# A decoder step on one core: the computed instruction order starts at the first instruction instead of at the second stage

## The chip, the cores and the metric

One Trainium2 chip, one core of it. The metric is the device time of one execution in microseconds; the median of three runs stands for a kernel. On the core five engines work at the same time, each on its own queue of instructions and in the order of that queue: TensorE (PE, with its weight loads as PEld), VectorE (DVE), ScalarE (ACT), GpSimd (POOL) and SyncE (SP), which here only issues transfers. An instruction that waits holds up everything behind it on its engine.

## The reference, cut to what matters

One layer of a hybrid decoder, for a prompt of 1024 rows and for a decode group of 8 x 8 rows that shares the weights. Only the first part matters for the change:

```
h = rmsnorm(x, norm_mix_pre)
z = h @ w_in                          # 1024 -> 256 + 256 + 32 + 512
c_q, c_kv, k_r, u = split(z)
attn = mla(c_q, c_kv, k_r)            # decode group: 8192 cached rows per sequence, read through a page table
ssm  = s5(u)                          # complex diagonal state space, parameters from ssm_a, ssm_log_dt, ssm_b, ssm_c
x = x + rmsnorm(concat(rmsnorm(attn), rmsnorm(ssm)) @ w_out)
x = x + cross_attention(x);  x = x + conv_ffn(x)
```

## The kernel before, in words

`Kern` runs its stages one after the other. `stage_in` (L396) is the projection z = h @ w_in. The rows are nine tiles, in the order 8 (the 64 decode rows), 0, 1, ..., 7 (128 prompt rows each, every eighth row). A tile's matmuls (L488) are 24 triples, 8 slices of the 1024 inputs by three products of high and low halves, into three PSUM banks of the tag "z", of which there are six. `rows_T` (L465) loads a tile ahead: xT, which ACT and DVE split into xh and xl (L325, L326), and x, which ACT squares and sums (L356) and POOL turns into the scale r1 (L345, L346). After the matmuls ACT scales z into cz (L490), DVE copies kr_raw and u_all (L496 to L499), and these free the three banks; then cn and ckv are written and stored.

Three other pieces of work sit between the tiles. At t == 1, `q_weights` (L544) loads w_uq in two parts (staging tile "wuq"), splits them into wuqh and wuql in a pool q_s opened for that, and `query_rows` (L552) makes the decode queries q_s. At t == 2, `dec_start` (L938) opens a pool d_q, reads the page table into the row indices idx, transposes w_uk (L959) and the queries (L968), multiplies them (L981) into Ql, sends Ql through DRAM (qld, L985, L987) into Qb, and closes d_q. From t == 3 to t == 7 two pieces a tile of `gen_ssm` (L610) are traced: the state space parameters, a long chain of small DVE operations on tiles of up to 128x256 that begins with the load of prm (L625) and ends with `yield True` (L752). All banks that these use are "z" banks too, and the six go round in the order in which the code asks for them.

`stage_par` (L1194) comes next. `gen_dec` (L1005) is the decode attention, 16 steps of two sequences' pages; a step gathers its cached rows with two DMAs that POOL issues (L1027, 2 MB each; tiles rf and kf, kf in turns in the buffers d_k0 and d_k1), DVE transposes blocks of them (kT, L1049), PE makes scores (S, L1060), DVE the maximum (mx, L1081), ACT the exponentials (P, L1088), PE the transposes and the values (L1109, L1125). Between its pieces `side()` runs the rest of the state space part, the gate, memory keys, prompt queries and weights.

Two things set the order. The tile framework places every instruction by its own simulated schedule. And `Order` (L60), made in `stage_par` at L1203, remembers how many instructions exist then; its `close()` (L220) takes all later ones up to the end of `stage_par`, derives their dependences, schedules them with a table of costs (`cost`, L104) in six rounds of a forward and a backward pass, and chains the instructions of PE, DVE, ACT and POOL in the best order found. SP's transfers are not chained. For the first use of each tile it also demands that the users of all pools listed in `behind` (L48) are through: closed pools of the same memory and the same side. `stage_in` lies outside of it.

Of the kernel before, what the change touches and what calls it, by code (L numbers as in the profile page):

```python
# [41 lines left out]
class Pool:  # L42


    def __init__(self, kern, pool, bufs, space, side):
        self.kern, self.pool, self.bufs = kern, pool, bufs
        self.space, self.open = (space, side), True
        self.behind = [p for p in kern.pools if not p.open and p.space == self.space]  # L48
        kern.pools.append(self)

    def tile(self, shape, dtype, **kw):
# [3 lines left out]

    def close(self):
        self.open = False


class Order:  # L60
# [238 lines left out]
class Kern:  # L299
# [95 lines left out]

    def stage_in(self):  # L396
        nc, i, o = self.nc, self.i, self.o
        self.pers = self.pool("pers", 1, self.actx)
        pers = self.pers
        self.u_all = pers.tile([128, 32, 8, 16], F32, tag="u_all", name="u_all")  # L400
# [64 lines left out]
        def rows_T(t):  # L465

            P = 64 if t == 8 else 128
            xT, x = first if t == 8 else (load_xT(t), load_x(t))
            j = sp.tile([128, D], BF16, tag="sqj", name="sqj", bufs=1)[:P]
            xh = sp.tile([128, 8, 128], F32R, tag="xh", name="xh")[:, :, :P]  # L470
            xl = sp.tile([128, 8, 128], F32R, tag="xl", name="xl")[:, :, :P]
            for k in (0, 4):
                self.split(xh[:, k:k + 4], xl[:, k:k + 4], xT[:, k:k + 4])
            r1 = self.rstd(sp, self.sumsq(sp, x, "ss1", j=j), D, "rs1")
            return r1, xh, xl

        order = (8, 0, 1, 2, 3, 4, 5, 6, 7)
        ahead = rows_T(8)
        for n, t in enumerate(order):
            P = 64 if t == 8 else 128  # L480
            r1, xh, xl = ahead
            if n < 8:
                ahead = rows_T(order[n + 1])
            zs = [zp.tile([128, 512], F32, tag="z", name="z") for _ in groups]
            for k in range(8):
                for (lhs, rhs, a, b) in ((xh, wh, k == 0, False), (xh, wl, False, False), (xl, wh, False, k == 7)):
                    for z, (c0, c1) in zip(zs, groups):
                        nc.tensor.matmul(z[:P, :c1 - c0], lhs[:, k, :P], rhs[:, k, c0:c1], start=a, stop=b)  # L488
            cz = sp.tile([128, 512], F32, tag="cz", name="cz")[:P]
            nc.scalar.activation(cz, zs[0][:P], AF.Copy, scale=r1)  # L490
            if t == 8:
                nc.vector.tensor_scalar_mul(kr_s_raw, zs[1][:64, 0:32], r1)
                nc.vector.tensor_scalar_mul(u_sn[:, 0:240], zs[1][:64, 32:272], r1)
                nc.vector.tensor_scalar_mul(u_sn[:, 240:512], zs[2][:64, :272], r1)
            else:
                nc.vector.tensor_scalar_mul(kr_raw[:, t], zs[1][:, 0:32], r1)  # L496
                grp = lambda a: a.rearrange("p (g c) -> p g c", c=16)
                nc.vector.tensor_scalar_mul(self.u_all[:, 0:15, t], grp(zs[1][:, 32:272]), r1)
                nc.vector.tensor_scalar_mul(self.u_all[:, 15:32, t], grp(zs[2][:, :272]), r1)  # L499
            ss2 = sp.tile([128, 2], F32, tag="ss2", name="ss2")[:P]  # L500
            j = sp.tile([128, 256], BF16, tag="sqc", name="sqc", bufs=1)[:P]
            self.sumsq(sp, cz[:, :256], "", ss2[:, 0:1], j)
            self.sumsq(sp, cz[:, 256:], "", ss2[:, 1:2], j)
            r2 = self.rstd(sp, ss2, 256, "rs2")
            cn = sp.tile([128, 512], F32, tag="cn", name="cn")[:P]
            nc.scalar.activation(cn[:, :256], cz[:, :256], AF.Copy, scale=r2[:, 0:1])
            ckv = self.ck_s if t == 8 else cn[:, 256:]
            natj = lambda a: a.rearrange("(c j) d -> j c d", j=8)[t]
            nc.vector.scalar_tensor_tensor(ckv, cz[:, 256:], r2[:, 1:2], g_kv[:P], op0=OP.mult, op1=OP.mult)
            if t == 8:  # L510
                nc.sync.dma_start(o["kv_s"], ckv)
                lat8 = cn, ckv
            else:
                nc.sync.dma_start(natj(o["kv_p"]), ckv)
                nc.sync.dma_start(natj(self.lat), cn)
                self.rope(sp, (kr_rot[:, t, 0:16], kr_rot[:, t, 16:32]), (kr_raw[:, t, 0:16], kr_raw[:, t, 16:32]),
                          csP[:, 0, t], csP[:, 1, t], [16])
            if t == 0:
                sample_lat(*lat8)
            if t == 1:  # L520

                qctx = ExitStack()
                qp = self.pool("q_s", 1, qctx, side="right")
                w = self.q_weights(qp, qp)
                self.q_s = pers.tile([64, 768], F32, tag="qy", name="q_s")
                self.query_rows(qp, [zp.tile([128, 512], F32, tag="z", name="z") for _ in range(2)], self.q_s,
                                self.cqTh_s, self.cqTl_s, *w, self.csS[:, 0], self.csS[:, 1])
                qctx.close()
            zbank = lambda: zp.tile([128, 512], F32, tag="z", name="z")
            if t == 2:  # L530
                self.dec_start(zbank)
                self.ssm_groups, opened = self.gen_ssm(zbank), False
            if 2 < t < 8:
                for _ in range(2):
                    opened = opened or next(self.ssm_groups)
        while not opened:
            opened = next(self.ssm_groups)
        nc.sync.dma_start(o["kr_p"].rearrange("(c j) r -> c j r", j=8), kr_rot)
# [1 line left out]
        self.dump("u_all", self.u_all)  # L540
        self.dump("u_sn", self.u_sn)


    def q_weights(self, wp, sp):  # L544
        wh, wl = (wp.tile([128, 2, 768], F32R, name="wuq" + z) for z in "hl")
        for k in range(2):
            st = sp.tile([128, 768], F32, tag="wuq", name="wuq", bufs=1)
            self.nc.sync.dma_start(st, self.i["w_uq"][k * 128:(k + 1) * 128])
            self.split_gain(wh[:, k], wl[:, k], st, self.col("q", k))
        return wh, wl  # L550
# [18 lines left out]
    def gen_q(self):  # L569

        nc, i = self.nc, self.i
        self.qd = self.pool("qd", 1, space=DRAM).tile([1024, 768], F32, name="qd")
        self.ckd = self.pool("ckd", 1, space=DRAM).tile([2, 128, 2, 1024], F32, name="ckd")
        ctx = ExitStack()
        sp = self.pool("q2_s", 1, ctx)
        pp = self.pool("q2_p", 2, ctx, space=PSUM)
        wh, wl = self.q_weights(sp, sp)
        bank = lambda: pp.tile([128, 512], F32, tag="ps", name="ps")
        csN = sp.tile([128, 2, 8, 16], F32, name="csN")
        nc.sync.dma_start(csN, i["k_rope_n"])  # L580
        yield
        for t in range(8):
            ts = slice(t * 128, (t + 1) * 128)
            lat = sp.tile([128, 4, 128], F32, tag="lat", name="lat", bufs=1)
            nc.sync.dma_start(lat.rearrange("p k n -> p (k n)"), self.lat[ts])
            ps = bank().rearrange("p (k n) -> p k n", k=4)
            for k in range(4):
                nc.tensor.transpose(ps[:, k], lat[:, k], self.ident)
            h, l = (sp.tile([128, 4, 128], F32R, tag="c" + z, name="c" + z, bufs=1) for z in "hl")
            self.split(h, l, ps)  # L590
            for z, a in ((0, h), (1, l)):
                nc.sync.dma_start(self.ckd[z, :, :, ts], a[:, 2:4].bitcast(F32))
            yield
            q = sp.tile([128, 768], F32, tag="q", name="q", bufs=2)
            self.query_rows(sp, (bank(), bank()), q, h, l, wh, wl, csN[:, 0, t], csN[:, 1, t])
            nc.sync.dma_start(self.qd[ts], q)
            yield
        ctx.close()
# [339 lines left out]
    def dec_start(self, bank):  # L938
# [1 line left out]
        nc, i = self.nc, self.i  # L940
        V, G = nc.vector, nc.gpsimd
        c1 = self.d_c
        ctx = ExitStack()
        sp = self.pool("d_q", 1, ctx, side="right")

        pt_i = sp.tile([128, 32], I32, name="pt_i")
        nc.sync.dma_start(pt_i, i["ptab"])
# [46 lines left out]
        ps = bank()  # L994
        nc.tensor.transpose(ps[:32, :64], self.kr_s, self.ident[:64, :64])
        V.tensor_copy(self.ckT_s[:, 8], ps[:32, :64])
        ctx.close()

    def stage_decopen(self):
        ctx = self.dctx  # L1000
# [193 lines left out]
    def stage_par(self):  # L1194

        def side():
            yield from self.ssm_groups
            yield from self.gen_glu()
            yield from self.gen_memkv()
            yield from self.gen_q()  # L1200
            yield from self.gen_attw()

        self.order = Order(self)  # L1203
        other = side()
        for _ in self.gen_dec():
            with self.tc.high_priority(100):
                next(other, None)
        for _ in other:
            pass
        self.order.close()  # L1210
        self.dctx.close()
# [1022 lines left out]
```

## Time and profile before

| | us |
|---|---|
| median of three runs (1981.37 to 1987.07) | 1987.0 |
| the profiled execution | 1987.95 |
| its span, first to last instruction | 1986.1 |
| PE busy in the span | 1846.4 |
| DVE busy | 1109.6 |
| ACT busy | 807.4 |
| POOL busy | 514.4 |

Busy time is an average over stages with different limits. In the windows below, PEclk is the TensorE clock that was granted, as a share of 2.4 GHz, and a busy PE at 0.5 does half as much. In a timeline row the bracket gives the idle time of the engine before the instruction and what ended it.

### The profile page before, as it was taken

Reading aid. Unit: us, or ns where it says so; the run is one execution under the profiler, and the core shown is the slowest. Engines: PE = TensorE matmul, PEld = TensorE weight load, DVE = VectorE, ACT = ScalarE, POOL = GpSimd, SP = SyncE. Lnnn points to the kernel's source line nnn. Section 1 sums busy time; section 2 is a strip of 40 time slices with the busy share of each in tenths; the row PEclk is TensorE's granted clock in tenths of the full one; section 3 lists DMA queues with packets and bytes.
Section 4 is the critical chain, followed back from the end, with each engine's and each line's share of the span. In section 5 each row is a group of like instructions: output and inputs, shape, how many; then the busy total and the mean of one; then the engine's idle time right before and its main releaser. Section 6 shows DMA issues by size and latency. Waiting matters only on the chain.

```text
span 1986.1 us, 31961 instructions
## 1 busy us (share of the span) xinstructions
PE 1846.4 (93%) x12675; PEld 1450.1 (73%) x12675; DVE 1109.6 (56%) x2013; ACT 807.4 (41%) x1598; POOL 514.4 (26%) x550
## 2 busy tenths in 40 slices
PE   8977898789899989999989989999999999999997
PEld 6864445346465578877868868888878999999776
DVE  4359889865646678864255563434544543334433
ACT  5232323234332368764254454333443333333342
POOL 2231111041130024234311023122144421110654
PEclk9887989899899999999999999999999999999999
DMA  7723533453575531231143352333333522222221
GB/s 239 224 72 116 203 113 130 169 214 130 192 271 204 200 94 28 78 137 50 43 138 117 138 191 95 98 101 98 97 105 106 165 86 86 86 85 79 75 85 59
DMA packets 136597, 248.07 MB, mean 125 GB/s; under 512 B 26912, under 2 KB 91232, under 8 KB 132352
## 3 DMA queue, kind: packets, MB, share of 16 engines
q1 hardware_dynamic: 129120, 170.01, 27.2%
q0 software_dynamic: 7328, 76.03, 10.0%
q8 instruction: 100, 1.64, 0.3%
q14 instruction: 49, 0.40, 0.1%
HBM read 217.26 MB, written 27.42 MB: 123 GB/s over the span
## 4 chain that ended last, share of the span: by engine, by line
PE 62%; ACT 2%; DVE 2%; issue 1%; POOL 1%; DMA 1%; SPq 0%; DVEq 0%; ACTq 0%; POOLq 0%
PE ps L2092 26%; PE z L1597 5%; PE ps L335 4%; PE ps L337 4%; PE ps L336 4%; PE b L1752 2%; PE t L1400 1%; PE S L1060 1%; PE ov L1125 1%; PE o L1416 1%; PE o L1417 1%; PE s L1378 1%; PE s L1379 1%; PE s L1380 1%; PE b L335 1%
## 5 line engine op out<-in xcount | busy, mean ns | idle before, releaser
L2092 PE MATMUL ps<-xTl,wh 128*128 128x288 f32 (+1 forms) x1056 | 287.9, 327 | 0.0
L2092 PE MATMUL ps<-xTh,wh 128*128 128x288 f32 (+1 forms) x1056 | 287.7, 327 | 0.0
L2092 PE MATMUL ps<-xTh,wl 128*128 128x288 f32 (+1 forms) x1056 | 287.7, 327 | 0.0
L326 POOL TENSOR_TENSOR wl<-st,wh 128x1024 fp32r<-128x1024 f32 (+1 forms) x52 | 116.7, 2245 | 408.0 <-ACT wh L325 397.7
L326 DVE TENSOR_TENSOR wl<-st,wh 128x1024 fp32r<-128x1024 f32 (+1 forms) x52 | 64.0, 1231 | 249.8 <-ACT wh L325 247.3
L325 ACT ACTIVATE wh<-st 128x1024 fp32r<-128x1024 f32 (+1 forms) x104 | 102.6, 993 | 235.4 <-PE ps L2092 215.2
L2092 PEld LDWEIGHTS ps<-xTl,wh 128*128 128x128 f32 x1056 | 179.6, 188 | 13.9
L2092 PEld LDWEIGHTS ps<-xTh,wl 128*128 128x128 f32 x1056 | 179.5, 188 | 13.8
L2092 PEld LDWEIGHTS ps<-xTh,wh 128*128 128x128 f32 x1056 | 179.6, 188 | 13.7
L1060 PE MATMUL S<-kT,Qb 32*64 32x512 f32 x2304 | 163.1, 641 | 27.0 <-DVE kT L1049 20.3
L326 DVE TENSOR_TENSOR wdl<-std,wdh 128x1024 fp32r<-128x1024 f32 x44 | 100.4, 2282 | 147.3 <-ACT wdh L325 147.3
L1049 DVE STREAM_TRANSPOSE kT<-kf 128x1024 f32<-128x1024 f32 x128 | 152.4, 1222 | 32.5 <-DMA kf<-in_cache_kv_dram,idx 22.9
L2043 POOL TENSOR_TENSOR al<-act,ah 128x1024 fp32r<-128x1024 f32 x44 | 106.8, 2428 | 174.0 <-ACT ah L2042 174.0
L335 PE MATMUL ps<-wdh,ah 128*128 128x512 f32 x352 | 139.5, 396 | 0.0
L336 PE MATMUL ps<-wdl,ah 128*128 128x512 f32 x352 | 139.1, 395 | 0.0
L1125 PE MATMUL ov<-kf,PT 128*64 128x256 f32 x1024 | 126.6, 394 | 0.7 <-ACT PT L1110 0.7
L337 PE MATMUL ps<-wdh,al 128*128 128x512 f32 x352 | 126.1, 396 | 0.0
L1125 PEld LDWEIGHTS ov<-kf,PT 128*64 128x64 f32 x1024 | 70.6, 141 | 54.6 <-issue 15.1
L1060 PEld LDWEIGHTS S<-kT,Qb 32*64 32x64 f32 x2304 | 46.6, 136 | 84.8 <-issue 40.0
L2042 ACT ACTIVATE ah<-act 128x1024 fp32r<-128x1024 f32 (+1 forms) x44 | 49.0, 1113 | 142.1 <-PE ps L336 136.9
L335 PEld LDWEIGHTS ps<-wdh,ah 128*128 128x128 f32 x352 | 66.2, 188 | 17.4 <-issue 0.8
L1027 POOL DMA_INDIRECT kf<-in_cache_kv_dram,idx x32 | 33.3, 1040 | 175.1 <-PE ov L1125 169.3
(536 smaller groups left out, 3945.9 us busy)
## 6 DMA issues: line engine op xcount, KB each, us to landing
st<-in_w_gate_dram SPq DMA_DIRECT2D x22, 1024.0 KB
st<-in_w_up_dram SPq DMA_DIRECT2D x22, 1024.0 KB
std<-in_w_down_dram SPq DMA_DIRECT2D x44, 512.0 KB
x<-in_x_prompt_dram SPq DMA_DIRECT2D x16, 512.0 KB
x<-x2d SPq DMA_DIRECT2D x15, 512.0 KB
wst<-in_w_in_dram SPq DMA_DIRECT2D x8, 528.0 KB
xT<-in_xT_dram SPq DMA_DIRECT2D x8, 512.0 KB
ws<-in_w_out_dram SPq DMA_DIRECT2D x8, 512.0 KB
```

The lines of the kernel that those rows point to most:

```text
L325: nc.scalar.activation(hi, src, AF.Copy)
L326: (lo_eng or nc.vector).tensor_sub(lo, src, hi.bitcast(F32))
L335: mm(ps, lh, rh, start=start, stop=False)
L336: mm(ps, lh, rl, start=False, stop=False)
L337: mm(ps, ll, rh, start=False, stop=stop)
L1049: V.transpose(t, RF[n] if kb == 8 else KF[n][:, :, :, kb * 32:kb * 32 + 32])
L1060: nc.tensor.matmul(SS[n][half[a], j], Qb[q, kb, 2 * p + a], ts[q, a], start=kb == BLOCKS[0], stop=kb == BLOCKS[-1])
L1125: nc.tensor.matmul(ov[half[a]], PTS[n, g][:, m, half[a]], KF[n][:, a, g * 4 + m], start=g == 0 and m == 0, stop=g == 3 and m == 3)
L1597: nc.tensor.matmul(z[n], l, r[:, n * 512:(n + 1) * 512], start=a, stop=b)
L2042: nc.scalar.activation(ah[:, :, :nt], a[:, :, :nt], AF.Copy)
L2043: G.tensor_sub(al, a[:, :, :512], ah[:, :, :512].bitcast(F32))
L2092: nc.tensor.matmul(zt[:, :c1 - c0], l[:, k], r[:, k, c0:c1], start=a, stop=b)
```

## The change

`self.order = Order(self)` moves from `stage_par` to the first line of `stage_in`, so that the computed order covers both stages. `behind` no longer looks at the side of a pool. A class `Slab` cuts tiles as slices out of one tile, and `slab()` asks for that tile in the buffer "kf" of pool d_k0, which the first gather of cached rows will fill later. The split query weights and all temporaries of `dec_start` now lie in such slabs, and pool d_q is gone. The staging of w_uq shares the one-buffer ring "x" with the row loads of `rows_T`. `gen_ssm` is created before the loop and gives one piece after every tile from the third on (n > 1, which is t == 1) in place of two after each from t == 3 on.

```
-        self.behind = [p for p in kern.pools if not p.open and p.space == self.space]
+        self.behind = [p for p in kern.pools if not p.open and p.space[0] == self.space[0]]
...
+class Slab:
+    def __init__(self, tile):
+        self.flat, self.off, self.tags = tile, 0, {}
+    def tile(self, shape, dtype, tag=None, name=None, bufs=1):
+        key, n = tag or name, math.prod(shape[1:])
+        if key not in self.tags:
+            self.tags[key] = self.flat[:shape[0], self.off:self.off + n]
+            self.off += n
...
     def stage_in(self):
+        self.order = Order(self)
...
+        zbank = lambda: zp.tile([128, 512], F32, tag="z", name="z")
+        self.ssm_groups, opened = self.gen_ssm(zbank), False
...
-                w = self.q_weights(qp, qp)
+                w = self.q_weights(self.slab(F32R), sp, "x")
...
-                self.ssm_groups, opened = self.gen_ssm(zbank), False
-            if 2 < t < 8:
-                for _ in range(2):
-                    opened = opened or next(self.ssm_groups)
+            if n > 1:
+                opened = opened or next(self.ssm_groups)
...
+    def slab(self, dtype=F32):
+        t = self.d_k[0].tile([128, 2, 16, 256], dtype, tag="kf", name="slab", bufs=1)
+        return Slab(t.rearrange("p a m r -> p (a m r)"))
...
-    def q_weights(self, wp, sp):
+    def q_weights(self, wp, sp, tag):
-            st = sp.tile([128, 768], F32, tag="wuq", name="wuq", bufs=1)
+            st = sp.tile([128, 1024], F32, tag=tag, name="wuq", bufs=1)[:, :768]
...
     def dec_start(self, bank):
-        ctx = ExitStack()
-        sp = self.pool("d_q", 1, ctx, side="right")
+        sp = self.slab()
...
-        ctx.close()
...
     def stage_par(self):
-        self.order = Order(self)
```

## Rows read from the trace of the kernel before

**Rows 1.** The page, section 1: busy us (share of the span) and instructions of each engine
```profile
PE 1846.4 (93%) x12675; PEld 1450.1 (73%) x12675; DVE 1109.6 (56%) x2013; ACT 807.4 (41%) x1598; POOL 514.4 (26%) x550
```

**Rows 2.** Windows, one a stage: length, busy us (instructions) of each engine, PEclk, DMA share, GB/s
```profile
0.00:140.50 140.50, 120.92 (x731) 106.35 (x731) 59.13 (x191) 54.03 (x107) 37.06 (x99) 0.94 0.58 182
140.50:697.00 556.50, 479.13 (x4773) 273.00 (x4772) 412.40 (x734) 181.77 (x449) 95.04 (x103) 0.92 0.49 175
697.00:1986.00 1289.00, 1246.34 (x7172) 1070.76 (x7172) 638.04 (x1091) 571.59 (x1043) 382.35 (x348) 0.99 0.30 97
```

**Rows 3.** Timeline of PE to 120 us: start, us, instruction, count, idle time before
```profile
8.42 1.14 PE L488 MATMUL z<-winh,xh 128*64 128x512 f32 x3 [8.42 <-ACT winh L330]
...
60.58 1.03 PE L959 MATMUL z<-ident,wuk 128*128 128x128 f32 x8
...
66.82 4.07 PE L981 MATMUL z<-qnT,wukT 64*128 64x64 f32 x29 [4.82 <-DVE qnT L971]
...
76.31 0.64 PE L488 MATMUL z<-winh,xh 128*128 128x512 f32 x3
76.79 0.65 PE L488 MATMUL z<-winl,xh 128*128 128x512 f32 x3
...
118.73 0.57 PE L488 MATMUL z<-winh,xh 128*128 128x272 f32 x1 [6.13 <-DVE u_all L498]
```

**Rows 4.** Timeline of ACT around 62 us
```profile
62.24 1.06 ACT L356 ACTIVATE sqj<-x 128x1024 bf16<-128x1024 f32 x1 [3.84 <-DMA x<-in_x_prompt_dram]
...
64.33 0.67 ACT L490 ACTIVATE cz<-z,rs 128x512 f32<-128x512 f32 x1
```

**Rows 5.** Windows about the three PE gaps and behind them, columns as before
```profile
61.90:75.80 13.90, 9.08 (x58) 8.35 (x57) 3.73 (x11) 6.31 (x15) 4.31 (x12) 0.63 0.97 358
...
112.60:123.50 10.90, 4.77 (x20) 4.58 (x20) 7.50 (x28) 3.54 (x9) 5.59 (x14) 0.69 0.05 17
...
140.50:149.07 8.57, 0.64 (x5) 0.45 (x5) 5.61 (x13) 3.33 (x10) 2.95 (x10) 0.68 0.39 115
149.07:176.40 27.33, 22.25 (x228) 12.53 (x228) 25.41 (x52) 2.50 (x7) 6.64 (x6) 0.60 0.53 185
176.40:360.00 183.60, 158.03 (x1638) 88.44 (x1638) 168.95 (x343) 60.61 (x167) 23.40 (x29) 0.93 0.40 143
```

**Rows 6.** Timeline of DVE, first and last operations of the parameter chain, first transposes
```profile
92.00 0.15 DVE L627 TENSOR_SCALAR nsgn<-prm 128x1 f32<-128x1 f32 x1 [19.85 <-DMA prm<-in_ssm_par_dram]
...
117.96 0.24 DVE L496 TENSOR_SCALAR kr_raw<-z,rs 128x32 f32<-128x32 f32 x1
...
147.69 1.24 DVE L1049 STREAM_TRANSPOSE kT<-rf 128x1024 f32<-128x1024 f32 x1
...
164.71 9.10 DVE L1049 STREAM_TRANSPOSE kT<-kf 128x1024 f32<-128x1024 f32 x8
```

**Rows 7.** Timeline of SP's transfers
```profile
71.97 0.37 SPq L985 DMA_DIRECT2D qld<-Ql  x1
79.66 1.80 SPq L987 DMA_DIRECT2D Qb<-qld  x4
81.56 0.65 SPq L625 DMA_DIRECT2D prm<-in_ssm_par_dram  x1
```

**Rows 8.** Timeline of POOL: a scale alone, the first kf gather's second half, a scale beside the chain
```profile
20.29 0.55 POOL L346 TENSOR_TENSOR rs<-rs1t,neghalf 128x1 f32<-128x1 f32 x1
...
62.26 0.94 POOL L1027 DMA_INDIRECT kf<-in_cache_kv_dram,idx  x1 [0.30 <-issue]
...
96.95 1.00 POOL L346 TENSOR_TENSOR rs<-rs1t,neghalf 128x1 f32<-128x1 f32 x1
```

**Rows 9.** Up to 720 us: a DVE wait (total, times, longest), kf's landing, the maxima
```profile
DVE kT L1049 <- DMA kf<-in_cache_kv_dram,idx: 22.9, 7, 6.1
...
DMA to landing us min/median/max: 8.1/12.9/15.2
...
L1081 DVE TENSOR_REDUCE mx<-S x16: 2252/2291/2293, 176.4 to 678.3; 128x1 f32<-128x2048 f32 x16
```

More of the change, by code (lines that the diff above doesn't have):

```diff
@@ L57, in close @@
         self.open = False
+class Slab:
[6 more added lines that the diff above has]
+            self.off += n
+            assert self.off <= self.flat.shape[1]
+        v = self.tags[key]
+        if len(shape) > 2:
+            dims = "abcd"[:len(shape) - 1]
+            v = v.rearrange(f"p ({' '.join(dims)}) -> p {' '.join(dims)}", **dict(zip(dims, shape[1:])))
+        return v if dtype == self.flat.dtype else v.bitcast(dtype)
 class Order:
@@ L528, in stage_in @@
                 qctx.close()
-            zbank = lambda: zp.tile([128, 512], F32, tag="z", name="z")
             if t == 2:
                 self.dec_start(zbank)
-                self.ssm_groups, opened = self.gen_ssm(zbank), False
-            if 2 < t < 8:
-                for _ in range(2):
-                    opened = opened or next(self.ssm_groups)
+            if n > 1:
+                opened = opened or next(self.ssm_groups)
         while not opened:
@@ L576, in gen_q @@
         pp = self.pool("q2_p", 2, ctx, space=PSUM)
-        wh, wl = self.q_weights(sp, sp)
+        wh, wl = self.q_weights(sp, sp, "wuq")
         bank = lambda: pp.tile([128, 512], F32, tag="ps", name="ps")
```

## The prediction

> **What bounds the kernel now.** I read the page first: PE is busy for 1846.4 of 1986.1 us and no other engine for more than 56% [rows 1]. So time is to be had only where PE stands idle or runs at the lower clock. Windows by stage then say where that is [rows 2]. Behind 697 us, where the change touches nothing, PE is idle for 43 of 1289 us at a clock of 0.99. The projection (to 140.5 us) leaves 19.6 us idle at 0.94, and the planned stage (140.5 to 697) leaves 77.4 us idle at 0.92. The change can win only in these two.
>
> The timeline of PE shows the projection's idle time as three pieces [rows 3]: 8.42 us at the start, until the first weights have come; 4.82 us ahead of 66.82; 6.13 us ahead of 118.73. A fourth lies at the seam: in the 8.57 us up to the first scores at 149.07 PE is busy for 0.64 [rows 5]. Behind a gap PE runs at the lower of its two levels, 1.2 and 2.4 GHz: the windows about the three gaps have a granted clock of 0.63, 0.69 and 0.68 [rows 5]. At the upper one a triple of the projection follows the next after 0.48 us, as at 76.31 and 76.79 [rows 3].
>
> Each gap has a reason in the order, not in a lack of data. At 62.24 ACT sums the squares of a row tile that is needed only much later, and waits 3.84 us for its load; the split xh and the scaling cz, which frees the bank, stand behind it on ACT, cz at 64.33 [rows 4], and on DVE the copies to wukT and qnT stand behind the xl that follows xh. At 118.73 PE waits for u_all: DVE takes up kr_raw only at 117.96, because the parameter chain, which could not begin before prm came at 92.00, is ahead of it [rows 6]. prm was issued at 81.56, behind Qb, which had waited for qld since 71.97 [rows 7]. At the seam DVE does parameter tables first and turns the first gathered block at 147.69 [rows 6]; the rows it turns were gathered at about 60 us [rows 8]. The plan could not know: it takes up at the seam and has the gather start there.
>
> **The change, part by part.** All sums are against the profiled execution, 1987.95 us; its span is 1986.1, so 1.85 us lie around it. It is 1 us above the median of 1987.0.
>
> *The gap at 62 us.* The plan now covers ACT and DVE here and knows that cz and qnT are due earlier than a square sum. Removed: 4.82 us of idle, and the half speed behind it. The 9.08 busy us of that window [rows 5] lie between 66.82 and 76.31 but for a little; at half speed they lose 4.5 us if all of it goes with the clock. The small products of 64 columns, 4.07 us and more of it [rows 3], may not, so the loss is 2.1 to 4.5 and I take 3.3. Sum 8.1. Not all goes: the six banks go round, so the fourth bank of `dec_start` needs tile 2's first bank, which cz frees in 0.67 us [rows 4], then the first product must be evacuated. I leave 1.5 us standing. Gain 6.6.
>
> *The gap at 118 us.* prm is now asked for at t == 1, before `dec_start`, a tile and all of `dec_start` earlier, and the chain, 26 us long from 92.00 to 117.96 with other work in it [rows 6], is spread over six tiles. Removed: 6.13 us, and behind it most of the window's 4.77 busy us at half speed [rows 5], 2.3. Gain 8.4. If DVE still held up one tile's copies, at most the same 8.4 would stay.
>
> *The seam.* The plan now has the gathered rows in place and the engines in their true state. The first block can be turned as soon as the last matmul gives up the projection's weights, in whose place the tile lies: u_all, one transpose of 1.24 us [rows 6] and the first scores, 2.5 us. Of the 7.9 idle us there [rows 5], 5.4 go.
>
> *Query weights through the ring "x".* Both loads now stand behind a square sum of 1.06 us [rows 4] and a load of x; an estimate from these is 2 to 5 us later. What they serve in the end, the work of `dec_start`, began on PE at 60.58, behind tile 2's matmuls [rows 3]. Cost nothing, since 11.6 us of tile 2 (24 triples of 0.48 us) cover it; without that cover it is us for us, 2 to 5 us.
>
> *The first kf gather moves behind `dec_start`.* Its buffer now holds the slabs until qld has read Ql. That transfer is waited for until 79.66 after its issue at 71.97 [rows 7], so with the gap gone the buffer is free at about 72 us instead of before 61. With two issues and the longest landing of 15.2 us [rows 9] the rows are there by 90, and the first use lies at 125 or later. Cost nothing, under 35 us of cover. While POOL waits for qld, the scales of the next tile queue behind it; a wrong guess of the plan costs them up to 7 us once, and the second set of three banks hides 11.6. I take nothing, bound 7.
>
> *The rest of the planned stage* is planned anew from another start. In the 27.33 us behind 149.07 PE was busy 22.25 us at a clock of 0.60 [rows 5], while the nine blocks of the first step waited: eight were turned only from 164.71 on [rows 6], though long there. If they go first, up to 5.1 us idle and 8.9 us of clock come back, 14 in all. But DVE was busy for 169 of the next 183.6 us [rows 5], so what is moved ahead there pushes other work back. I take nothing, and bound it by a gain of 14 and by the losses below.
>
> Sum: 6.6 + 8.4 + 5.4 = 20.4 us. The profile would then show 1967.5, the median 1967.
>
> *One rule against the change.* The scale of a tile takes POOL 0.55 us at 20.29 and 1.00 us at 96.95, beside the chain on DVE [rows 8], and the chain will now lie beside six tiles. The Trainium skill, page "SBUF — State Buffer", section "Who interferes with whom", says that a VectorE instruction with two SBUF inputs contends with a GpSimd instruction that reads SBUF, and that the second to issue fully blocks; the trace agrees in direction, by 0.45 us an operation. If every tile's two scales and one rotary step stretch by 0.45 us on the path, six tiles lose 8 us and the median would be 1975. I hold it for unlikely, since r1 is made a tile ahead.
>
> **The rivals.** *The planned order is no tighter than the framework's* (also the case that the change does not do what it says). For: in the stretch that is planned now, PE is idle for 13.9% of the time (77.4 of 556.5), in the projection after its start for 8.5% (11.2 of 132.1) [rows 2, 3]. At 13.9% the projection's 120.9 busy us would take 140.4 instead of 132.1; with the seam's 5.4 us won, the kernel would be 3 us slower, 1990. Against: the planned stretch is idle where DVE is full or a gather lands, and the projection has neither.
>
> *The whole planned stage gets better too*, because the first step's blocks go first: 20.4 + 14, 1953.
>
> *Slower: gathers come into the open.* A gather takes 8.1 to 15.2 us to land and DVE waited for one in 7 steps, 22.9 us together, the longest 6.1 [rows 9]. If decode steps are packed more tightly ahead of the side work, a step shortens towards its gather. At 6.1 us in 10 of the 15 later steps the waits are 61 us, 38 more than now, less 20 won: 2005. It decides from 7 steps at 6.1 us, or 13 at the mean of 3.3, where it has eaten the 20 us. Against: the plan knows the transfers' length, and a step is 33.5 us long in the mean (15 steps from 176.4 to 678.3) [rows 9].
>
> **How the numbers follow.** Forecast 1967: 0.50. Better stage, 1953: 0.15. POOL held up, 1975: 0.05. No tighter, 1990 or somewhat below: 0.16. Slower, 2005: 0.14. About 0.3%, 6 us, is what a measurement of this kernel can tell from no change. Faster takes the first three, 0.70; same 0.16; slower 0.14. The range reaches down past the better case by the upper ends of the bounds, 1.2 us more lost clock at the first gap and the 1.5 and 2.5 us that I left standing, and up past the no-tighter case: 1947 to 1991. The slower case stays outside, and so does what is better than all bounds.
>
> **What would show it.** Right: the last projection matmul ends between 122 and 130 us; no PE gap over 3 us between 9 us and there; prm lands before 60; the first scores follow the last projection matmul within 4 us; the stage ends near 677. Wrong: POOL idle on the first kf gather with scales behind it; ACT waiting for a load again with cz behind it; decode steps of which most wait for kf; or a projection that ends at 125 while the stage still ends near 697, which would say that the second stage's end hangs on something else than its start.

## The result and the profile after

The kernel after takes 1955.56 us in the median of six runs (1952.82 to 1968.35), the kernel before 1985.15 beside it (1979.34 to 1991.38): a ratio of 0.9853, 95% interval 0.9833 to 0.9873. Two later series of the unchanged kernel after gave 0.9844 and 0.9872 (below), so the change is worth 25 to 31 us. The forecast was 1967. The profiled execution of after took 1952.82 us, its span is 1951.0. The page's first section:

```profile
PE 1837.9 (94%) x12675; PEld 1442.3 (74%) x12675; DVE 1105.0 (57%) x2013; ACT 806.9 (41%) x1598; POOL 522.5 (27%) x550
```

PE does the same 12675 matmuls in 8.5 us less than in [rows 1], and is idle for 113 us in place of 140. Windows cut at the same two places as [rows 2], the last projection matmul and the transfer of krd that ends the planned stage (columns as there):

```profile
0.00:138.40 138.40, 121.92 (x731) 105.85 (x731) 61.12 (x194) 55.50 (x113) 38.21 (x103) 0.95 0.59 186
138.40:664.50 526.10, 469.31 (x4772) 266.34 (x4772) 406.18 (x727) 180.11 (x442) 103.45 (x100) 0.94 0.52 185
664.50:1950.90 1286.40, 1246.67 (x7172) 1070.09 (x7172) 637.74 (x1094) 571.33 (x1043) 380.86 (x348) 0.99 0.31 97
```

The projection, from which 15 us were to come, is 2.1 us shorter (140.5 to 138.4). The second stage, from which 5.4 were to come at the seam (the place where the projection ends and the planned stage begins), is 30 us shorter (556.5 to 526.1); two more profiles of after have 538.5 and 535.7 for it, and the mean of the three gives 23 us in place of 30. In the last, 1289.0 and 1286.4 us, PE's busy time is the same.

**The projection.** The timeline of PE, with the rows before which it waited and those at the seam:

```profile
7.87 1.14 PE L510 MATMUL z<-winh,xh 128*64 128x512 f32 x3 [7.87 <-ACT winh L349]
28.93 0.69 PE L510 MATMUL z<-winh,xh 128*64 128x512 f32 x3 [2.37 <-ACT winh L349]
30.29 0.88 PE L510 MATMUL z<-winl,xh 128*64 128x512 f32 x3 [0.66 <-DVE winl L350]
72.78 4.06 PE L1004 MATMUL z<-slab 64*128 64x64 f32 x29 [4.65 <-DVE slab L994]
138.07 0.29 PE L510 MATMUL z<-winh,xl 128*128 128x272 f32 x1
138.95 0.66 PE L812 MATMUL ps<-ident,u_all 128*128 128x128 f32 x4 [0.59 <-DVE u_all L521]
141.28 0.64 PE L1082 MATMUL S<-kT,Qb 32*64 32x512 f32 x1
```

Beside [rows 3]: the wait of 6.13 us for u_all is gone. The wait of 4.82 us ahead of the products with w_uk is still there with 4.65, six microseconds later. And 3.0 us of waiting for the first weights' split are new, at 28.93 and 30.29.

The wait of 4.65 us ends with a copy of DVE, the queries' from a PSUM bank into the slab (L994). PE's transposes of the queries, which that copy reads, and DVE's operations from the first parameter operation to the copy:

```profile
66.70 0.46 PE L991 MATMUL z<-ident,slab 64*128 64x64 f32 x4
```

```profile
63.65 0.18 DVE L668 TENSOR_SCALAR ek<-prm 128x32 f32<-128x32 f32 x1 [2.01 <-DMA prm<-in_ssm_par_dram]
...
69.77 0.29 DVE L700 TENSOR_SCALAR wide<-wide 128x256 f32<-128x256 f32 x1
69.97 0.25 DVE L518 TENSOR_SCALAR kr_raw<-z,rs 128x32 f32<-128x32 f32 x1
...
70.52 0.68 DVE L983 COPY slab<-z 128x512 f32<-128x512 f32 x1
...
72.32 0.41 DVE L994 COPY slab<-z 128x256 f32<-128x256 f32 x1
```

The transposes are through at 67.16. DVE works on the parameter chain from 63.65 to 70.06 without a pause, and the copies come behind it, the last at 72.32. So the parameter chain, which an earlier prm has brought to this place, holds up the products here. ACT's timeline shows the pattern of [rows 4] again, square sums that wait for a load, but none of them is what PE waits for:

```profile
54.19 1.06 ACT L375 ACTIVATE sqj<-x 128x1024 bf16<-128x1024 f32 x1 [4.90 <-DMA x<-in_x_prompt_dram]
...
66.87 1.06 ACT L375 ACTIVATE sqj<-x 128x1024 bf16<-128x1024 f32 x1 [5.78 <-DMA x<-in_x_prompt_dram]
...
71.82 1.06 ACT L375 ACTIVATE sqj<-x 128x1024 bf16<-128x1024 f32 x1 [2.76 <-DMA x<-in_x_prompt_dram]
...
72.87 0.67 ACT L512 ACTIVATE cz<-z,rs 128x512 f32<-128x512 f32 x1
```

The three wait 13.4 us together, and the cz behind the last begins at 72.87, when the products have begun (72.78).

**The seam.** DVE's timeline from the first block that it turns to the first maximum:

```profile
138.81 1.24 DVE L1071 STREAM_TRANSPOSE kT<-rf 128x1024 f32<-128x1024 f32 x1
139.97 2.33 DVE L1071 STREAM_TRANSPOSE kT<-kf 128x1024 f32<-128x1024 f32 x2
...
142.59 1.24 DVE L1071 STREAM_TRANSPOSE kT<-kf 128x1024 f32<-128x1024 f32 x1
...
155.90 2.27 DVE L1103 TENSOR_REDUCE mx<-S 128x1 f32<-128x2048 f32 x1
```

and SP's and POOL's, the issue of the load of the parameters and the first gather of kf:

```profile
60.92 0.45 SPq L649 DMA_DIRECT2D prm<-in_ssm_par_dram  x1
...
82.26 1.06 POOL L1049 DMA_INDIRECT kf<-in_cache_kv_dram,idx  x1 [5.84 <-DVE ey L678]
```

Gathered blocks are turned from 138.81 on, between the parameter tables; in [rows 6] the tables went first and the blocks waited until 164.71. So the first scores come 2.9 us behind the last projection matmul (8.6 before), and the first maximum 17.5 us behind it, where 176.4 in [rows 9] is 35.9 behind 140.5. Windows about this, the first two to be read beside the third and fourth of [rows 5], the last beside its fifth:

```profile
138.40:141.28 2.88, 2.33 (x37) 2.16 (x38) 2.88 (x4) 0.95 (x2) 2.23 (x7) 1.00 0.79 223
141.28:155.90 14.62, 11.68 (x175) 5.18 (x173) 14.62 (x27) 2.12 (x7) 3.99 (x6) 1.00 0.90 332
155.90:339.50 183.60, 160.30 (x1670) 88.82 (x1678) 181.04 (x376) 61.90 (x169) 36.42 (x31) 0.90 0.43 152
```

From the first scores to the first maximum it is 14.6 us in place of 27.3, at a clock of 1.00 in place of 0.60. In the 183.6 us behind the maximum DVE is busy for 181.0 us, before for 169.0.

### The profile page after: what moved, and what is told of

Same layout as the page of the kernel before. It is cut to its first block, busy times and chain, and to the rows that moved or that the text cites. A ratio compares the mean times of both kernels' runs of the same rounds, so it can differ in the third digit from the quotient of the medians.

```text
span 1951.0 us, 31948 instructions
## 1 busy us (share of the span) xinstructions
PE 1837.9 (94%) x12675; PEld 1442.3 (74%) x12675; DVE 1105.0 (57%) x2013; ACT 806.9 (41%) x1598; POOL 522.5 (27%) x550
## 5 line engine op out<-in xcount | busy, mean ns | idle before, releaser
L1082 PE MATMUL S<-kT,Qb 32*64 32x512 f32 x2304 | 155.0, 635 | 14.7 <-DVE kT L1071 8.8
L1071 DVE STREAM_TRANSPOSE kT<-kf 128x1024 f32<-128x1024 f32 x128 | 152.5, 1221 | 28.7 <-DMA kf<-in_cache_kv_dram,idx 19.2
L1147 PE MATMUL ov<-kf,PT 128*64 128x256 f32 x1024 | 131.0, 404 | 0.6 <-ACT PT L1132 0.6
L1082 PEld LDWEIGHTS S<-kT,Qb 32*64 32x64 f32 x2304 | 42.5, 135 | 66.7 <-issue 32.4
```

Of the source, the lines that this page charges most:

```text
L1071: V.transpose(t, RF[n] if kb == 8 else KF[n][:, :, :, kb * 32:kb * 32 + 32])
L1082: nc.tensor.matmul(SS[n][half[a], j], Qb[q, kb, 2 * p + a], ts[q, a], start=kb == BLOCKS[0], stop=kb == BLOCKS[-1])
L1147: nc.tensor.matmul(ov[half[a]], PTS[n, g][:, m, half[a]], KF[n][:, a, g * 4 + m], start=g == 0 and m == 0, stop=g == 3 and m == 3)
```

## The experiments

Each ratio is to the kernel before on the same chip. The milestones are read from the timelines of the profiled executions: the end of the last projection matmul; how far behind it the first scores and the first maximum begin; its distance to the transfer of krd; and from there to the end of the span. A plan here is one order that `Order` has computed. Each profile is a single execution: par_only's was the shortest of its ten, par_late's and before_r4's the longest of theirs. One execution of a plan differs from the next by up to 12 us in the second stage, as the three of after show, so small differences of that column say nothing.

The last column is read from the order in which PE, DVE, ACT and POOL run the instructions behind the transfer of krd, code that no edit touches. Over the fourteen profiles there are four such orders, here A to D.

| kernel | ratio, 95% interval | projection ends | scores | maximum | second stage | rest | its order |
|---|---|---|---|---|---|---|---|
| before | 1 | 140.5 | +8.6 | +35.9 | 556.0 | 1289.5 | B |
| after | 0.9853 [0.9833, 0.9873] | 138.4 | +2.9 | +17.5 | 526.2 | 1286.5 | A |
| after_again | 0.9844 [0.9812, 0.9875] | 137.3 | +2.9 | +17.5 | 538.5 | 1289.2 | A |
| after_third | 0.9872 [0.9833, 0.9911] | 137.0 | +2.9 | +17.5 | 535.7 | 1287.9 | A |
| par_only | 0.9935 [0.9908, 0.9961] | 131.7 | +8.5 | +35.8 | 547.5 | 1288.1 | A |
| par_late | 0.9927 [0.9904, 0.9950] | 131.6 | +8.5 | +35.8 | 564.7 | 1288.9 | A |
| two_orders | 0.9934 [0.9908, 0.9961] | 133.0 | +7.0 | +34.3 | 559.2 | 1292.7 | B |
| known_rows | 0.9960 [0.9928, 0.9991] | 143.2 | +4.6 | +22.2 | 538.2 | 1291.5 | D |
| par_known | 0.9894 [0.9862, 0.9927] | 133.1 | +4.6 | +20.9 | 542.3 | 1295.5 | C |
| par_known_too | 0.9901 [0.9864, 0.9937] | 132.0 | +4.6 | +21.5 | 536.1 | 1295.7 | C |
| own_ring | 0.9872 [0.9822, 0.9923] | 133.0 | +2.5 | +17.5 | 531.5 | 1295.3 | C |
| own_ring_r12 | 0.9847 [0.9805, 0.9888] | 135.1 | +2.5 | +17.5 | 528.8 | 1292.6 | A |
| after_r12 | 0.9890 [0.9861, 0.9919] | 136.2 | +2.9 | +17.6 | 528.3 | 1293.0 | A |
| before_r4 | 0.9984 [0.9961, 1.0007] | 143.8 | +8.7 | +36.0 | 563.0 | 1292.6 | D |

The second stage falls into two groups. It takes 526 to 542 us in the nine profiles whose plan has the first gathered rows in place (after and its variants with own_ring or twelve rounds, known_rows, par_known), and 547 to 565 in the five others, with the old layout or the new one.

**The new layout without the wider order: par_only.** The kernel after, with the order made where it was:

```
     def stage_in(self):
-        self.order = Order(self)
...
     def stage_par(self):
+        self.order = Order(self)
```

> The changed kernel with the computed order taken up at the seam again; slabs, the shared ring and the spread parameter pieces stay. Theory 1, the plan must know what is already gathered: the second stage is as before (556 us from the last projection matmul to the last transfer of the stage), the total 1983 give or take 4. Theory 2, the projection's order and the layout made the gain: the total stays near 1957. If the spread parameter pieces alone close the gap at 118 us, the last projection matmul comes at about 132 instead of 140.5 and the total is 1976.

About half of the whole gain is there already, and the projection, in the framework's own order, is shorter than in any planned one. PE's waits up to 145 us (total, times, longest), and DVE's turning of the first step's blocks:

```profile
PE z L509 <- ACT winh L349: 7.7, 1, 7.7
PE S L1081 <- DVE kT L1070: 7.2, 1, 7.2
PE z L1003 <- DVE slab L993: 2.1, 1, 2.1
```

```profile
155.79 9.10 DVE L1070 STREAM_TRANSPOSE kT<-kf 128x1024 f32<-128x1024 f32 x8
```

Both gaps of [rows 3] have gone or shrunk (none for u_all in the projection, 2.1 for 4.82), with nothing planned. What makes the second one shorter than in after is DVE's order: here the copies go into the parameter chain and not behind it. PE's transposes, and DVE's timeline:

```profile
63.19 0.46 PE L990 MATMUL z<-ident,slab 64*128 64x64 f32 x4
```

```profile
62.99 0.18 DVE L677 TENSOR_SCALAR ey<-ey 128x32 f32<-128x32 f32 x1
63.08 0.24 DVE L517 TENSOR_SCALAR kr_raw<-z,rs 128x32 f32<-128x32 f32 x1
...
65.33 0.41 DVE L993 COPY slab<-z 128x256 f32<-128x256 f32 x1
65.66 0.17 DVE L677 TENSOR_SCALAR ey<-ey 128x32 f32<-128x32 f32 x1
```

The last copy begins 1.7 us behind the end of the transposes, in after 5.2. The seam is as before.

**Which part of the layout: par_late.** par_only, with the parameter pieces again two a tile from t == 3 on:

```
-            if n > 1:
-                opened = opened or next(self.ssm_groups)
+            if 2 < t < 8:
+                for _ in range(2):
+                    opened = opened or next(self.ssm_groups)
```

> Planned from the seam, with slabs, but the parameter pieces again two a tile from the fourth prompt tile on. If the spread of the pieces closed the gap at 118 us, it comes back: PE waits for u_all for about 6 us, the last projection matmul at 138 to 140 instead of 131.7, ratio 0.998. If the slabs did it (prm no longer behind Qb), the projection stays at 132 and the ratio at 0.9935.

The same time and the same end of the projection, so spreading the pieces does nothing that can be measured. SP's timeline shows why the gap is gone anyway:

```profile
52.93 0.42 SPq L649 DMA_DIRECT2D prm<-in_ssm_par_dram  x1
...
71.27 0.36 SPq L1008 DMA_DIRECT2D qld<-slab  x1
...
76.92 1.81 SPq L1010 DMA_DIRECT2D Qb<-qld  x4
```

Though asked for late, prm is issued 28 us earlier than in [rows 7] and no longer behind Qb. What differs from the kernel before is that d_q is gone, that `dec_start` and the split query weights work in slabs, that the staging shares the ring "x", and that `behind` looks at both sides. That the memory of d_q held the load back is the likely reason, but it was not isolated.

**Two orders that know nothing of each other: two_orders.** The kernel after, with the first order closed at the end of `stage_in` and a second one made in `stage_par`:

```
     def stage_in(self):
...
+        self.order.close()
...
     def stage_par(self):
+        self.order = Order(self)
```

> The changed kernel with two plans: one for the projection, closed at the seam, and one from the seam on that knows nothing of the first. Theory 1 (what the joint plan knows at the seam): last projection matmul as in the changed kernel, 138, second stage as before, 556, total 1983 give or take 4. Theory 2 (the planned projection): near 1957.

A planned projection adds nothing to par_only (0.9934 and 0.9935), and the late first maximum is back (+34.3). What the wider order brings therefore comes through the seam.

**Only the knowledge: known_rows.** The kernel before, in which the planner is told that the first four gathers, those of step 0, are as good as landed. The table of costs alone is changed:

```
+            if type(x).__name__ == "InstDMACopy" and eng[k] == "Pool":
+                gathers += 1
+                if gathers <= 4:
+                    busy, end, nbytes = 1.0, 1.0, 0
```

> The kernel before with one edit in its planner: the first four gathers of the planned stage (rows of step 0) cost nothing and land at once in the plan, as they have in fact landed. Theory 1: step 0's transposes go first, the first maximum comes 18 us earlier behind the seam and the second stage is 18 to 30 us shorter, total 1956 to 1968. Theory 2: no gain, 1985. Theory 3 (any other plan gives another time, by chance): anything within 15 us of 1985, with the first maximum where it was.

With layout and projection as before it gains 0.4%, 8 us, by the ratio (the two medians of that series, 1979.77 and 1994.25, lie 14 us apart), less than the 18 to 30 that were expected of it, and DVE's timeline turns blocks at once:

```profile
146.44 1.23 DVE L1053 STREAM_TRANSPOSE kT<-rf 128x1024 f32<-128x1024 f32 x1
147.60 2.32 DVE L1053 STREAM_TRANSPOSE kT<-kf 128x1024 f32<-128x1024 f32 x2
...
165.44 2.27 DVE L1085 TENSOR_REDUCE mx<-S 128x1 f32<-128x2048 f32 x1
```

The first maximum is 13.7 us nearer to the last projection matmul than in the kernel before; the projection itself came out 2.7 us longer in this plan. In its profile the second stage is 17.8 us shorter (538.2 for 556.0), and 4.7 of them go to the longer projection and a rest that is 2.0 longer.

**A control for chance in a plan: before_r4.** The kernel before with ROUNDS = 4 for 6, which gives another order of nearly the same worth.

> The kernel before with four rounds of planning in place of six: another order of nearly the same quality by the planner's own account (2 us longer), and nothing else. A control for the chance in a plan: if plans that the planner holds alike run alike, the ratio is 0.999 to 1.003; if an order drawn anew moves the time by as much as the 0.4% that the told rows gave, the ratio lies outside of 0.997 to 1.004, and that gain can't be put down to the knowledge.

0.9984, inside of the wider bounds and outside of the narrower. An order drawn anew moved the time by 0.16%, with an interval that holds no change, against 0.40% for the told rows. The intervals of the two overlap, so this control alone would not do. The milestones and the next pair carry it: the control's first maximum stays at +36.0, where the told rows bring it to +22.2, and the untouched code behind has the same order in both (D).

**Layout and knowledge together: par_known, par_known_too.** par_only with the lines of known_rows, in two series.

> The plan is taken up at the seam as before, with the slabs and the spread pieces, and it is told that the rows of step 0 have landed (their four gathers cost nothing in it). Theory 1, all that the joint plan brings behind the seam is this knowledge: last projection matmul at 132, first maximum 18 to 22 us behind it, ratio 0.985 or less, as the changed kernel. Theory 4, planning both stages together brings more: ratio 0.989 to 0.990 (the 0.9935 of the kernel planned from the seam, less the 0.4% that the knowledge gave the kernel before).

> The projection as the framework orders it, the plan from the second stage on with the first four gathers told as landed, unchanged from the earlier run of it (0.9894). Theory J: 0.989 to 0.991, 6 us or more above the kernel after. Theory K: within 4 us of it.

0.9894 and 0.9901, 0.3 to 0.4% below par_only and par_late. The gain of the knowledge is there on the new layout too, and the ratios show about half of it or less. The transfer of krd comes at 675.4 and 668.2 us, in par_only and par_late at 679.2 and 696.2: 16 us earlier in the mean. But the rest, 1288.1 and 1288.9 us there, takes 1295.5 and 1295.7 here, in another order of its instructions (C in place of A), and so 7 us are lost again behind the planned stage.

**The kernel after again, beside these: after_again, after_third.**

> The changed kernel itself, unchanged, on the chip of the next three: 0.985 of the kernel before. Its second profile shows how far two executions of one plan lie apart; if the stage behind the seam differs by more than 5 us from 526, differences of that size between plans say nothing.

> The kernel after, unchanged, beside the next kernel on the same chip. Theory J (one joint plan from the first instruction is worth something beyond the knowledge that the first rows have landed): its median lies at least 6 us below that of the next kernel. Theory K (what the plan gained is only that knowledge, and the 0.45% between 0.985 and 0.989 in the earlier runs were chance): the two lie within 4 us of each other, near 0.987 both.

In the two series the medians of after lie 6.8 and 7.7 us below those of par_known (1963.95 and 1970.70; 1962.47 and 1970.17). The intervals overlap, but the two differences agree, and the reading that there is nothing beyond the knowledge allowed 4. The profiles place the difference where it was not looked for. The transfer of krd comes at 671.0 us in the mean of three profiles of after and at 671.8 in two of par_known: planning both stages as one brings nothing up to there. The rest takes 1287.9 and 1295.6. Its PE windows from 430 to 490 us behind krd, the end of the cross attention, for after_third and for par_known_too:

```profile
1102.69:1162.69 60.00, 53.08 (x278) 42.72 (x277) 37.20 (x60) 27.42 (x63) 13.94 (x24) 0.94 0.59 192
```

```profile
1098.16:1158.16 60.00, 51.10 (x293) 40.87 (x292) 37.34 (x61) 27.00 (x65) 14.24 (x24) 0.89 0.55 178
```

and in the same order the first matmul of the feed-forward part in PE's timeline:

```profile
1154.30 0.77 PE L2113 MATMUL ps<-xTh,wh 128*128 128x512 f32 x1
```

```profile
1157.61 0.77 PE L2117 MATMUL ps<-xTh,wh 128*128 128x512 f32 x1 [2.43 <-DVE pt L1512]
```

The feed-forward part begins 481.6 us behind krd in the one and 489.5 in the other. No line of that code was edited, but the two run it in different orders, A and C. The wait of 2.43 us ahead of the feed-forward part stands, at 2.43 to 2.44 us, in all five profiles with order C or D, and in none of the nine with A or B. So what the kernel after has over par_known here is the order that the framework gave to the untouched code, which par_only and par_late have as well (1288.1 and 1288.9); it isn't what the wider plan computes.

**The query weights off the ring "x": own_ring.** The kernel after, with w_uq staged in the buffer that the gathers of "rf" fill later:

```
-                w = self.q_weights(self.slab(F32R), sp, "x")
+                w = self.q_weights(self.slab(F32R), self.d_k[0], "rf")
...
-            st = sp.tile([128, 1024], F32, tag=tag, name="wuq", bufs=1)[:, :768]
+            st = sp.tile([128, 2, 16, 32], F32, tag=tag, name="wuq", bufs=1).rearrange("p a m e -> p (a m e)")[:, :768]
```

> The changed kernel with the staging of the query weights in the still empty buffer rf instead of the ring of the row loads. If that ring holds up ACT (loads of x waited for, with the scaling behind them), the 4.7 us gap at 72.8 us goes or shrinks below 2, the query products come at 47 instead of 52 us, the last projection matmul at about 131, total 1948. If the gap has another cause (DVE's parameter chain ahead of the copies), it stays and the total is 1953 to 1957.

PE's first query matmul, and the products with w_uk:

```profile
49.09 0.39 PE L582 MATMUL z<-slab,cqTh_s 128*64 128x512 f32 x1
...
68.50 3.70 PE L1004 MATMUL z<-slab 64*128 64x64 f32 x29 [3.90 <-DVE slab L994]
```

They come 3.2 and 4.3 us earlier than in after (the query matmul at 52.32 there, at 46.94 before), and the projection ends 4.6 us earlier than the mean of the three profiles of after. But the wait ahead of the products stays, 3.90 us, and with it the other cause that was named for it ahead of this run: DVE's parameter chain ahead of the copies. It runs from 59.31 to 65.29 here, and the copies begin at 65.74, though the transposes of the queries are through at 64.16. The time does not follow: 0.9872. The second stage is as long as in after (531.5, mean of after 533.5), and the rest again takes 1295.3, with the same wait of 2.43 us ahead of the feed-forward part. The order behind the planned stages is C, that of par_known. Why the framework's schedule gives one order or the other is not shown.

**More rounds of planning: after_r12 and own_ring_r12.** ROUNDS = 12 for 6, alone and with the edit of own_ring.

> The changed kernel with 12 rounds of planning instead of 6: another plan of the same work, which the planner itself holds for 3 us shorter. If the plan's own number is followed: 3 us below the changed kernel, within its noise. If plans of this kind scatter by chance, up to 10 us off in either direction.

> The kernel after with the query weights staged outside of the ring x, and with twelve rounds of planning. If the 5 us that the shared ring cost the projection reach the end, about 1956, some 5 us under the kernel after; if what is ahead of the next stage is given back there, as the earlier run of the first edit alone had it (0.9872), within 4 us of it.

Neither is shown to be faster than after. own_ring_r12, the fastest in its series, lies 2.9 us below after in the median (1959.61 and 1962.47), inside of both intervals; it is no proof of a version that beats both. after_r12 and own_ring_r12 have the order of after in everything behind the planned stages and still took 1293.0 and 1292.6 there. About 3 of these 5 us are lost in one stretch, 178 to 245 us behind krd; for after_third and for after_r12:

```profile
850.69:917.69 67.00, 62.91 (x305) 48.99 (x305) 26.10 (x43) 30.48 (x61) 30.12 (x46) 0.97 0.37 134
```

```profile
842.49:909.49 67.00, 63.22 (x297) 49.21 (x297) 24.68 (x42) 29.62 (x60) 26.25 (x43) 0.92 0.38 134
```

PE is busy for as long in both and gets less done, at a granted clock of 0.92 (in own_ring_r12 too) in place of 0.97. Why the clock is lower there stays open.

## Why the prediction was right in size and wrong in its terms

20.4 us were forecast and 25 to 31 measured, about 28, so the direction and about the size held. Of the three terms one held. By the mean of after's three profiles the projection gave 2.9 us for 15.0, the seam 5.7 for 5.4, the rest of the planned stage 16.8 for nothing, and the code behind 1.6. That the sum came near is luck in this: a term taken at nothing made up for the ones that failed.

*The gap at 62 us (6.6 forecast, 0.2 found).* The step that failed is "the plan now covers ACT and DVE here and knows that cz and qnT are due earlier than a square sum". What stands ahead of the copy of qnT is no longer a square sum but the parameter chain on DVE: the copies come at 70.52 to 72.73, behind the chain, though PE's transposes were through at 67.16, and PE waits 4.65 us for 4.82. So the two gaps were not two separate terms: the early prm that closes the one at 118 us feeds this one. The framework's order with the same early prm puts the copies into the chain (par_only, 2.1 us of waiting). Why the plan puts them behind it is not shown.

*The gap at 118 us (8.4 forecast).* It closed, but not for the reason given: par_late closes it with the pieces asked for at t == 3. And the projection as a whole gave 2.1 us. In idle time: 6.1 us less there, 0.2 less ahead of the products with w_uk and 0.6 less at the start; 3.0 more at 28.93 and 30.29, and 0.7 more in small pieces. That makes 3.1 us less idle (19.6 to 16.5), and PE's busy time went up by 1.0 where 2.3 of lost clock were to come back. The last matmul, forecast between 122 and 130 us, comes at 138.4, and prm, forecast to land before 60, is used at 63.65.

*The rival "no tighter than the framework's"* was right for the projection: 137.0 to 138.4 as planned in after, 131.6 and 131.7 in the framework's order with the same layout, worse by 6 us. A projection planned by itself (two_orders) ends at 133.0. The rival had a chance of 0.16 as the outcome of the whole. Wrong in it was that nothing else would make up for it.

*The ring "x" (cost 0, bound 2 to 5).* The step "11.6 us of tile 2 cover it" failed in the planned order. Against own_ring it costs the projection of after 4.6 us, inside of the bound; with twelve rounds of planning 1.1 (136.2 and 135.1). In the framework's order the projection ends at 131.7 with the same ring; what it would be there without was not run.

*The seam (5.4 forecast).* 8.57 to 2.88 us, 5.7: right, in size and in reason; known_rows has 4.0 of it from the knowledge alone. The stage's end, forecast near 677, comes at 664.5 to 675.8 in three profiles.

*The rest of the planned stage (0 taken, bound a gain of 14).* This is the term that carried the result. The first maximum follows the first scores 12.7 us sooner. The step that failed is "what is moved ahead there pushes other work back. I take nothing". It does push work back, and the room for it stood in the same row: DVE was busy for 169 of 183.6 us [rows 5], so 14.6 us were free; after, 2.6 are. DVE is busy for 12 us more there, which is where the work can have gone. From the first to the last maximum it takes 496 us in the mean of three profiles of after (489.2, 501.5, 498.7) and 501.9 before, so in these profiles nothing of the 12.7 us was given back later. The rival "whole stage better too", 1953, had this mechanism and its price; its chance of 0.15 was too low, and its other terms were as wrong as mine.

*What was taken at nothing and cost nothing.* The first kf gather is issued at 82.26 and used at 139.97: covered. POOL stood 5.84 us before it, for a DVE operation and not for qld, with qld through by 81.02, when Qb is issued, and no scale that PE waited for was behind it. Of the decode steps 6 wait for kf, 19.2 us together, the longest 6.2 (7, 22.9 and 6.1 in [rows 9]): gathers did not come into the open.

*The rule on the memory port* would have cost 8 us, for scales beside the parameter chain. Four tiles' scales on POOL took 1.07, 0.56, 0.54 and 0.54 us in after, at 73.62, 93.83, 104.20 and 116.64. Only the first is as long as the one that [rows 8] call "beside the chain", and the traces show something else beside both: the split xl, which reads two tiles of 128x512. In the kernel before (POOL's row at 96.95) and in after:

```profile
96.15 1.39 DVE L326 TENSOR_TENSOR xl<-xT,xh 128x512 fp32r<-128x512 f32 x2
```

```profile
72.98 1.28 DVE L345 TENSOR_TENSOR xl<-xT,xh 128x512 fp32r<-128x512 f32 x2
73.62 1.07 POOL L365 TENSOR_TENSOR rs<-rs1t,neghalf 128x1 f32<-128x1 f32 x1 [2.15 <-ACT cz L512]
...
92.47 1.32 DVE L345 TENSOR_TENSOR xl<-xT,xh 128x512 fp32r<-128x512 f32 x2
92.57 0.67 POOL L389 TENSOR_TENSOR kr_rot<-rp,rp 128x16 f32<-128x16 f32 x1
```

The rotary step at 92.57 takes 0.67 us beside xl and 0.21 at 103.84, where DVE is idle. The Trainium skill, page "SBUF — State Buffer", section "Who interferes with whom", says that a VectorE instruction with two SBUF inputs contends with a GpSimd instruction that reads SBUF; these rows agree with it. The splits are there in both kernels, so spreading the chain was no reason for a new cost, and none of PE's waits in the projection of after ends with POOL.

So of the 28 us, by the milestones of before and the mean of after's three profiles, 3 come in the projection, 22 to 23 in the second stage and 1 to 2 behind it. The 3 are what the planned order leaves of the 9 that the new layout gives to the projection in the framework's order (par_only, par_late: 131.7 and 131.6 for 140.5; 13 to 14 us of the whole by their ratios). The gain in the second stage goes with the knowledge that the first rows have landed: it is there in every plan that has it and in none that doesn't, and it comes with four told gathers alone, on the old layout and on the new. The 7 us by which after beats par_known are no gain over before, whose rest takes 1289.5: par_known loses them in order C.

## What to carry to other kernels

A planner that takes up in the middle of a kernel must be given the state at that point, what has landed and what is free; telling it that four gathers were done gained 8 us with four lines, and 16 us up to the end of the planned stage on the new layout. Before work that is moved ahead on a nearly full engine is priced at nothing, its idle time in the same window is the room for what is pushed back, and it is read directly from the row. When an edit brings a load forward, look at what the work that it sets free will now stand ahead of; here a chain of small operations, 28 us earlier than before, stood ahead of copies that PE waited for. When a change of layout and a change of order come together, the layout alone is the first experiment. And when an experiment is to be read by its total, compare the order of the code behind it too.

## What was not expected of the chip and its schedule

Executions of one and the same order differ more than the medians suggest: six of after_again took 1950.6 to 1966.8 us, and the planned second stage 526.2, 538.5 and 535.7 us in three profiles. The sixth decode step differs most, 39.7, 43.5 and 44.2 us; in the two longer ones PE waits 1.9 and 3.1 us for the transfer of a table, W, in the first it doesn't. The landing of kf ranged from 8.0 to 22.0 us in the first profile of after (8.1 to 15.2 before).

Code that nobody edits moves by 7 us. From the transfer of krd to the end it takes 1286.5 to 1289.2 us in five profiles with order A and 1295.3 to 1295.7 in three with order C, over three kernels that differ ahead of it only. One order alone varies as well: two more profiles with A took 1292.6 and 1293.0, at a lower granted clock in one stretch.
